# TensorE in program order in a banded attention loop, with background work shared out by key tiles

## The chip, the cores and the metric

The kernel runs on one core of a Trainium2 chip. The metric is the device time of one execution in microseconds; three runs were timed, and one more was profiled.

## The reference

The reference is a backbone of four layers over 512 latent and 256 context tokens of width 1024. Layer 1, where the change lies, is a banded grouped-query attention: 16 heads of 64 in 4 groups with shared keys and values, a window of 128 tokens to either side, and a sink logit for each head. Latent tokens see the band and all context tokens; context tokens see the context alone.

```python
mask = (jnp.abs(qpos[:, None] - kpos[None, :]) <= B_WINDOW) & (kpos[None, :] >= 0) & (kpos[None, :] < n)
s_band = jnp.einsum('bqhgd,bkhd->bhgqk', qi, kb).astype(jnp.float32) * scale
s_band = jnp.where(mask, s_band, NEG_INF)
s_ctx = jnp.einsum('bqhgd,bkhd->bhgqk', qi, k_c).astype(jnp.float32) * scale
return sink_attend([s_ctx, s_band], [v_c, vb], sink_l)
...
y_x = (o_x * jax.nn.silu(gate_x)) @ w_out
```

Each layer also has shift, scale and gate vectors, made by a 1024 x 3072 product of a conditioning vector (`mx = cond_x @ w_mod[layer] + b_mod[layer]`).

## The kernel before

All products run in float32 with operands split in a high and a low part, so that one product is two or three matmuls. The program is written with a planner: instructions are recorded in program order, and when the program is closed the planner simulates time and sets the order on each engine. On the chip each engine then works strictly in its own order.

`layer_B` first makes keys and values, and then loops over 96 units. A unit is one head and one block of 128 queries. There are 4 groups, 2 pairs of heads in each, 6 blocks, 2 heads of the pair: `n // 12` is the round `c`, so a round is one pair of heads over all six blocks. A latent block sees 4 or 5 key tiles of 128 (blocks 0 and 3: 4, blocks 1 and 2: 5), a context block (4 and 5) sees 2. In unit n, in this order in the program:

- `scores` of unit n + 2 (AH = 2): window scores (L1159) and masks (L1164), context scores (L1169) into one of two PSUM pairs; then on VectorE a reduce (L1174), on ScalarE the exponential with its sum (L1175), on VectorE reciprocal (L1176) and scale (L1177).
- `turn` of unit n: transposes (L1191) into one of three PSUM banks called short, then `split_ps`: ScalarE copies the high part (L337), VectorE subtracts the low part (L338).
- for the second head of a pair, `mix`: the product with the values (L1204), high parts first and then low parts, followed by two copies on ScalarE (L1207, L1208), two sums on VectorE (L1209, L1210) and a product on GpSimd (L1212).

Between these, `carry` advances a generator of background work for later rounds, before and after each `turn`: query projections (L1095) with their transposes (L1105), gate projections (L1076), and one filler per round from `CN`. A filler is a unit of the modulation product: four groups of four matmuls (L438), each group on its own 512 KB transfer from `w_mod`, then a copy on ScalarE (L469), transposes (L473) and small VectorE work (L477 to L483). The stream of these transfers (issued at L207) takes a buffer when an older one is free: in rounds 0 to 5 the first two groups of a filler have their weights loaded long ahead, and the transfers for the third and the fourth group wait on the queue until the first and the second group have been read. All background work uses one PSUM bank (called long, `pa0`), so the next piece must wait until the last one's bank has been read.

The steps of background work come from

```python
RATE = (5, 5, 5, 5, 5, 5, 5, 5)
...
carry(RATE[c] * 0.5)
turn(g, b, hh, prs.pop(0))
carry(RATE[c] * 0.5)
```

so five steps for each unit, whatever its size; rounds 0 to 5 have 47 to 49 steps.

Of the kernel before, what the change touches and what calls it, by code (L numbers as in the profile page):

```python
# [12 lines left out]
F32 = mybir.dt.float32  # L13
F32R = mybir.dt.float32r
BF16 = mybir.dt.bfloat16
AF = mybir.ActivationFunctionType
# [3 lines left out]
P = 128  # L20
# [11 lines left out]
CH = ((0, 384),)  # L32
LS = 2
WD = 3
RATE = (5, 5, 5, 5, 5, 5, 5, 5)
CN = (1, 1, 1, 1, 1, 1, 0, 9)
BK = (4, 5)
MI = (4, 8, 12, 16)
# [93 lines left out]
class Ring:  # L132
# [6 lines left out]
    def next(self):  # L139
        self.i += 1  # L140
        return self.blocks[self.i % len(self.blocks)]
# [125 lines left out]
class Kern:  # L267
# [761 lines left out]
    def layer_B(self, L, j, h, last):  # L1029
        nc, io = self.nc, self.io  # L1030
# [11 lines left out]
        BL = [1, 0, 2, 3, 4, 5]  # L1042
# [5 lines left out]
        qv = q.v(4, T)  # L1048
# [5 lines left out]
        wide, long, short = Banks(banks[0:BK[0]]), Banks(banks[BK[0]:BK[1]]), Banks(banks[BK[1]:8])  # L1054

        def taken(nm):
            ws = [self.W.take((nm, kb)) for kb in range(2)]
            return ws, lambda k: tuple(x[:, k % 4] for x in ws[k // 4][1])

        def roped(ps, t):  # L1060

            src = ps[:, 0:256].rearrange("p (h c) -> p h c", h=4)
            if t >= 4:
                return src
            rf = self.ropes.next().v(4, 64)
            self.rope_ps(rf, src, t, 4)
            return rf

        def gate(c):

            blk, (wh, wl) = self.W.take(("gate", c))
            for t0, n in spans:
                o = long.next()[:, 0:n]
                for k in range(KD):
                    for i, (l, part) in enumerate(((wh, 0), (wh, 1), (wl, 0))):
                        nc.tensor.matmul(o, l[:, k], self.h_at(h, part, k, t0, n), start=(k == 0 and i == 0), stop=(k == KD - 1 and i == 2))  # L1076
                    if k < KD - 1:
                        yield
                if t0:
                    blk.free()  # L1080
                self.gate2(ogv[:, c, t0:t0 + n], o)
                yield

        held, done = {}, []

        def query(g, t):

            if t == BL[0]:
                held[g] = taken(f"q{g}")
            ws, wk = held[g]  # L1090
            ps = long.next()
            for k in range(KD):
                wh, wl = wk(k)
                for i, (part, w) in enumerate(((0, wh), (0, wl), (1, wh))):
                    nc.tensor.matmul(ps[:, 0:256], self.h_at(h, part, k, P * t, P), w, start=(k == 0 and i == 0), stop=(k == KD - 1 and i == 2))  # L1095
                if k < KD - 1:
                    yield
            src = roped(ps, t)
            st = small.next()
            sv = st.v(4, 2, 64)  # L1100
            nc.scalar.activation(sv[:, :, 0], src, AF.Copy, scale=-0.125)
            nc.vector.scalar_tensor_tensor(sv[:, :, 1], src, -0.125, sv[:, :, 0].bitcast(F32), op0=ALU.mult, op1=ALU.subtract)  # L1102
            pt = short.next()
            for i in range(4):
                nc.tensor.transpose(pt[:, P * i:P * i + P], st.v(4, P)[:, i].bitcast(F32), self.ident)  # L1105
            nc.scalar.activation(qv[:, :, P * t:P * t + P], pt.rearrange("p (h n) -> p h n", h=4), AF.Copy)
            if t == BL[-1]:
                done.append(g)
                for blk, _ in ws:
                    blk.free()  # L1110
            yield

        def keys():

# [29 lines left out]
        def window(b):  # L1144
            return (max(0, b - 1), min(3, b + 1) + 1) if b < 4 else (0, 0)
# [36 lines left out]
        def turn(g, b, hh, pr):  # L1182
            lo, hi = window(b)
            nk = hi - lo + 2
            if hh % 2 == 0:
                ptl[0] = pts.next().v(2, 5, 256)
            ptv = ptl[0]
            for i0, n in ((0, 3), (3, 2)) if nk == 5 else ((0, nk),):
                tp = short.next()
                for i in range(n):  # L1190
                    nc.tensor.transpose(tp[:, P * i:P * i + P], pr.ap[:, P * (i0 + i):P * (i0 + i) + P], self.ident)  # L1191
                c0 = P * (hh % 2)
                self.split_ps(ptv[:, 0, i0:i0 + n, c0:c0 + P], ptv[:, 1, i0:i0 + n, c0:c0 + P],
                              tp[:, 0:P * n].rearrange("p (k n) -> p k n", k=n))
# [21 lines left out]
        def background(c):  # L1216

            g = (c + 1) // 2
            gates = gate(c + 1) if c < 7 else iter(())
            for i in range(3):  # L1220
                if g < 4:
                    yield from query(g, BL[i if c % 2 else i + 3])
                if c % 2:
                    for _ in range(KD):
                        if next(gates, 1) != 1:
                            yield
            yield from gates
            left = CN[c]
            while left and self.fillers and (self.fillers[0][0] == "ab" or self.fillers[0][1] == L):
                yield from self.unit(long.next)  # L1230
                left -= 1

        for x in [gate(0)] + [query(0, BL[i]) for i in range(3)]:
            for _ in x:
                pass
        units = [(g, b, 2 * p + i) for g in range(4) for p in range(2) for b in range(6) for i in range(2)]
        ahead = AH
        prs = [scores(*u) for u in units[:ahead]]
        debt = 0.0

        def carry(steps):
            nonlocal debt
            debt += steps
            while debt >= 1:
                debt -= 1
                next(back, None)

        for n, (g, b, hh) in enumerate(units):
            c = n // 12
            if n % 12 == 0:  # L1250
                back = background(c)
                debt = 0.0
                if c == 7:
                    assert done == [0, 1, 2, 3]
                    for x in h:
                        x.free()
                    self.ropes.free()
                    self.M.cap_d = self.M.look_d = 2
                    self.W.cap_w, self.W.cap_d = 8, 1
            if n + ahead < len(units):  # L1260
                prs.append(scores(*units[n + ahead]))
            carry(RATE[c] * 0.5)
            turn(g, b, hh, prs.pop(0))
            carry(RATE[c] * 0.5)
            if hh % 2:
                mix(g, b, hh // 2)
            if n % 12 == 11:
                assert next(back, 1) == 1, c
            self.W.pump(*((8, 8) if c == 7 else (3, 2)))
        for r in (small, pts, prob, sums):  # L1270
            r.free()
        for x in (q, kx, vb):
# [552 lines left out]
```

## Time and profile before

| what | value |
|---|---|
| median of three runs | 1970.33 us (1959.76 to 1973.29) |
| profiled execution | 1957.76 us |
| its span | 1956.0 us |
| TensorE busy | 1820.0 us (93%) |
| banded attention loop | 674 to 1016 us of the span |
| TensorE busy in the loop | 312.9 of 342 us |
| mean granted TensorE clock | 0.988 |

The span is the time from the first to the last instruction of the execution that the profiler recorded. Times inside the loop are counted from the span's start. PE is TensorE's matmuls, PEld its weight loads, DVE VectorE, ACT ScalarE, POOL GpSimd, SP the queue that issues transfers. The ends of matmuls are modelled, so that a matmul's row lasts longer than its share of the engine, and a wait shorter than the difference does not show.

### The profile page before, as it was taken

The numbers are of one execution on the slowest core, as the hardware profiler recorded it, in microseconds if no ns is written. First come the engines' busy times: TensorE is split into PE (matmuls) and PEld (weight loads), VectorE is DVE, ScalarE is ACT, GpSimd is POOL, SyncE is SP. The second block draws the span as 40 slices with busy tenths as digits, with TensorE's granted clock in tenths as the row PEclk, the third lists the DMA queues.
The fourth block names the chain that finished last, engine by engine and source line by source line (L and its number), as shares of the span: only waits on it lengthen the run. The fifth ranks groups of instructions, "written<-read, shape, count | busy, mean of one in ns | idle before, by whom it ended". The sixth has DMA issues, their size and how long they took to land. (4 is left out here: it accounts for less than half of the span.)

```text
span 1956.0 us, 30330 instructions
## 1 busy us (share of the span) xinstructions
PE 1820.0 (93%) x11628; PEld 1575.7 (81%) x11628; DVE 1176.2 (60%) x2364; ACT 813.0 (42%) x1694; POOL 521.9 (27%) x523
## 2 busy tenths in 40 slices
PE   5878999999999999999989899999998998999998
PEld 3657688999988878887858699999987777889986
DVE  6694225777746376667755455556667553477663
ACT  3473223545634255555653422222222353354451
POOL 5561000000314322222221444444444221000120
PEclk9999999999999999999989999999998999999999
DMA  7965541011222121222363622222222234310121
GB/s 221 264 181 156 163 130 32 13 33 33 78 96 87 55 76 54 76 77 87 100 202 112 195 69 69 85 76 70 73 76 93 88 118 138 102 34 22 44 76 54
DMA packets 186357, 186.32 MB, mean 95 GB/s; under 512 B 16600, under 2 KB 164952, under 8 KB 186212
## 3 DMA queue, kind: packets, MB, share of 16 engines
q1 hardware_dynamic: 186212, 184.39, 30.6%
q8 instruction: 91, 1.49, 0.3%
q14 instruction: 54, 0.44, 0.1%
HBM read 160.24 MB, written 24.12 MB: 94 GB/s over the span
## 5 line engine op out<-in xcount | busy, mean ns | idle before, releaser
L611 PE MATMUL pb<-arena_r 128*128 128x512 f32 (+1 forms) x1536 | 291.5, 344 | 7.3 <-DVE arena_f L1525 3.6
L611 PEld LDWEIGHTS pb<-arena_r 128*128 128x128 f32 x1536 | 238.4, 191 | 39.1 <-issue 4.5
L337 ACT ACTIVATE arena_r<-pa 128x384 fp32r<-128x384 f32 (+2 forms) x382 | 174.8, 479 | 208.6 <-PE pa L925 68.5
L338 DVE TENSOR_TENSOR arena_r<-pa,arena_r 128x384 fp32r<-128x384 f32 (+2 forms) x382 | 199.5, 537 | 96.8 <-ACT arena_r L337 95.1
L611 PE MATMUL pa<-arena_r,swing_R 128*128 128x512 f32 (+1 forms) x816 | 166.8, 356 | 1.1 <-ACT arena_f L454 0.5
L611 PEld LDWEIGHTS pa<-arena_r,swing_R 128*128 128x128 f32 x816 | 132.1, 188 | 25.2 <-issue 1.6
L900 PE MATMUL pb<-arena_r 128*128 128x384 f32 (+1 forms) x720 | 141.5, 337 | 3.0 <-ACT arena_r L337 1.8
L691 POOL TENSOR_TENSOR arena_f<-arena_f 128x128 f32<-128x128 f32 (+1 forms) x44 | 20.8, 473 | 408.6 <-DVE arena_f L690 223.4
L229 POOL TENSOR_TENSOR swing_R<-arena_f,swing_R 128x1024 fp32r<-128x1024 f32 (+1 forms) x33 | 76.1, 2311 | 187.3 <-ACT swing_R L226 133.1
L900 PEld LDWEIGHTS pb<-arena_r 128*128 128x128 f32 x720 | 119.0, 189 | 5.1 <-ACT arena_r L337 2.5
L645 PE MATMUL pb<-arena_r 128*128 128x512 f32 x480 | 116.6, 395 | 0.0
L645 PEld LDWEIGHTS pb<-arena_r 128*128 128x128 f32 x480 | 89.4, 188 | 21.5 <-issue 2.8
L354 POOL TENSOR_SCALAR small<-small 128x1 f32<-128x1 f32 x68 | 18.6, 274 | 326.1 <-ACT trash L587 136.6
L229 POOL TENSOR_TENSOR arena_r<-swing_F,arena_r 128x1024 fp32r<-128x1024 f32 x34 | 84.4, 2483 | 74.0 <-ACT arena_r L226 73.9
L939 PE MATMUL pa<-arena_r 128*128 128x256 f32 x624 | 91.4, 287 | 2.1 <-DVE arena_r L338 2.1
L939 PEld LDWEIGHTS pa<-arena_r 128*128 128x128 f32 x624 | 81.8, 190 | 4.7 <-ACT arena_r L337 2.5
L1095 PE MATMUL pa<-swing_R,arena_r 128*128 128x256 f32 x576 | 77.2, 285 | 3.8 <-DVE arena_f L344 2.0
L904 DVE TENSOR_REDUCE small<-pb 128x1 f32<-128x768 f32 (+1 forms) x80 | 67.5, 846 | 21.6 <-PE pb L900 20.8
L907 ACT ACTIVATE arena_f<-pb,small 128x768 f32<-128x768 f32 (+1 forms) x80 | 65.2, 816 | 33.0 <-DVE small L905 26.6
L226 ACT ACTIVATE arena_r<-swing_F 128x1024 fp32r<-128x1024 f32 x35 | 37.2, 1063 | 93.8 <-PE pb L611 86.7
L1095 PEld LDWEIGHTS pa<-swing_R,arena_r 128*128 128x128 f32 x576 | 71.0, 189 | 5.2 <-DVE arena_f L344 2.4
L1076 PE MATMUL pa<-arena_r,swing_R 128*128 128x512 f32 (+1 forms) x384 | 73.4, 341 | 1.6 <-DVE arena_r L1102 1.4
(270 smaller groups left out, 4220.3 us busy)
## 6 DMA issues: line engine op xcount, KB each, us to landing
arena_f<-in_w_mod_dram SPq DMA_DIRECT2D x93, 512.0 KB, 4.7
swing_F<-in_c_w_in_dram SPq DMA_DIRECT2D x31, 512.0 KB, 4.0
kd<-arena_f SPq DMA_DIRECT2D x48, 256.0 KB, 3.4
arena_f<-in_a_w_in_dram SPq DMA_DIRECT2D x24, 512.0 KB, 4.3
arena_f<-kd SPq DMA_DIRECT2D x16, 768.0 KB, 4.5
arena_f<-in_b_w_in_dram SPq DMA_DIRECT2D x20, 512.0 KB, 3.8
x<-arena_f SPq DMA_DIRECT2D x18, 512.0 KB, 3.3
arena_f<-in_a_w_out_dram SPq DMA_DIRECT2D x16, 512.0 KB
```

The source lines that it names most:

```text
L226: nc.scalar.activation(hi, view, AF.Copy)
L229: eng.tensor_tensor(lo, view, hi.bitcast(F32), op=ALU.subtract)
L337: self.nc.scalar.activation(hi, src, AF.Copy)
L338: self.nc.vector.tensor_tensor(lo, src, hi.bitcast(F32), op=ALU.subtract)
L611: nc.tensor.matmul(out, l, rhs(part, k, i), start=(k == 0 and q == 0), stop=(k == kt - 1 and q == 2))
L645: nc.tensor.matmul(ys[:, 512 * hf:512 * hf + 512], ov[:, part, k], wt[:, 0, 512 * hf:512 * hf + 512], start=(k == 0 and q == 0), stop=(k = ...
L900: nc.tensor.matmul(S[:, 512 * b:512 * b + w], l, r[:, k0 + w * b:k0 + w * b + w], start=(q == 0), stop=(q == 4))
L904: nc.vector.tensor_reduce(mx, Sv, axis=AX.XY, op=ALU.max)
L907: nc.scalar.activation(pr.v(nb, w), Sv, AF.Exp, bias=mx, scale=sc, accum_out=sm)
L939: nc.tensor.matmul(o[:, 0:256], vv[:, a_, kt % 3, P * hh:P * hh + P], ptv[i // nh][:, b_, i % nh], start=(i == 0 and q == 0), stop=(i == n ...
L1076: nc.tensor.matmul(o, l[:, k], self.h_at(h, part, k, t0, n), start=(k == 0 and i == 0), stop=(k == KD - 1 and i == 2))
L1095: nc.tensor.matmul(ps[:, 0:256], self.h_at(h, part, k, P * t, P), w, start=(k == 0 and i == 0), stop=(k == KD - 1 and i == 2))
```

## The change

Four things change in `layer_B`.

1. The loop over the units is put into a region in which the planner keeps TensorE's instructions in program order. The other engines and the queues are planned as before.
2. The steps of background work in a unit are proportional to its key tiles: `rate` is the number of steps of the round divided by 44, the sum of key tiles over its units. What is left after the last unit of a round is drained there.
3. A step that ends with work on the background's bank yields "rest", and `carry` then stops until its next call. What it owes is kept.
4. The transposes and the copy of a query tile are held back by four steps of background (`DEFER`).

```diff
-RATE = (5, 5, 5, 5, 5, 5, 5, 5)
+DEFER = 4
...
                 self.gate2(ogv[:, c, t0:t0 + n], o)
-                yield
+                yield "rest"
...
-            yield
+
+            def turned():
+                pt = short.next()
+                for i in range(4):
+                    nc.tensor.transpose(pt[:, P * i:P * i + P], st.v(4, P)[:, i].bitcast(F32), self.ident)
+                nc.scalar.activation(qv[:, :, P * t:P * t + P], pt.rearrange("p (h n) -> p h n", h=4), AF.Copy)
+                if t == BL[-1]:
+                    done.append(g)
+
+            yield turned
...
                 yield from self.unit(long.next)
+                yield "rest"
                 left -= 1
 
+        def deferred(steps):
+
+            late = []
+            for x in steps:
+                late = [(k - 1, f) for k, f in late]
+                while late and late[0][0] <= 0:
+                    late.pop(0)[1]()
+                if callable(x):
+                    late.append((DEFER, x))
+                    x = "rest"
+                yield x
+            for _, f in late:
+                f()
+                yield
...
             while debt >= 1:
                 debt -= 1
-                next(back, None)
-
+                if next(back, None) == "rest":
+                    break
+
+        order_pe = self.tc.manual_schedule(engines={nc.tensor.engine})
+        order_pe.__enter__()
         for n, (g, b, hh) in enumerate(units):
             c = n // 12
             if n % 12 == 0:
-                back = background(c)
+                back = deferred(background(c))
                 debt = 0.0
+                rate = (24 * (c < 7) + 16 * (c < 7) + 7 * (CN[c] > 0) + 2) / 44
...
-            carry(RATE[c] * 0.5)
+            share = rate * (window(b)[1] - window(b)[0] + 2) * 0.5
+            carry(share)
             turn(g, b, hh, prs.pop(0))
-            carry(RATE[c] * 0.5)
+            carry(share)
...
             if n % 12 == 11:
-                assert next(back, 1) == 1, c
+                for _ in back:
+                    pass
...
+        order_pe.__exit__(None, None, None)
```

The lines of the loop move down by four (L1163 is the old L1159, L1173 the old L1169, L1195 the old L1191, L1208 the old L1204, L1179 the old L1175, L1211 and L1212 the old L1207 and L1208); the query transposes go from L1105 to L1110 and their copy from L1106 to L1111.

TensorE over the filler of round 3, before. L438 is a filler group of four matmuls (x8 is two groups), L1169 context scores, L1159 and L1164 window scores and masks, L1191 transposes of the probabilities, L1105 transposes of queries:

```order
L438 MATMUL pa_65<-arena_f,cst 32x256 x8
L1169 MATMUL pb_70<-arena_r 128x256 x2
L1159 MATMUL pb_69<-arena_r 128x256
L1164 LDWEIGHTS identb
L1164 MATMUL pb_69<-maskb,identb 128x128
L1159 MATMUL pb_69<-arena_r 128x256
L1191 MATMUL pa_67<-ident,arena_f 128x128 x2
L1105 MATMUL pa_68<-ident,arena_r 128x128 x4
L1169 MATMUL pb_69<-arena_r 128x256 x2
L438 MATMUL pa_65<-arena_f,cst 32x256 x4
L1191 MATMUL pa_68<-ident,arena_f 128x128 x2
L438 MATMUL pa_65<-arena_f,cst 32x256 x4
```

The same place in the changed kernel, from the first group on:

```order
L438 MATMUL pa_65<-arena_f,cst 32x256 x4
L1195 MATMUL pa_66<-ident,arena_f 128x128 x2
L438 MATMUL pa_65<-arena_f,cst 32x256 x4
L1173 MATMUL pb_69<-arena_r 128x256 x2
L438 MATMUL pa_65<-arena_f,cst 32x256 x4
L1195 MATMUL pa_67<-ident,arena_f 128x128 x2
L438 MATMUL pa_65<-arena_f,cst 32x256 x4
L1110 MATMUL pa_68<-ident,arena_r 128x128 x4
L1208 MATMUL pa_66<-arena_r 128x256 x4
```

The four groups now stand one to a step, with two pairs of transposes and one pair of context scores between the first and the last; the window scores of the next round and the query transposes, which stood among them, come after the fourth group.

TensorE at the end of round 3 in the kernel before, from the scores of the second head of the next round's block 0 to the mix (L1204) of block 5. L473 are the filler's transposes, L1095 query projections:

```order
L1169 MATMUL pb_70<-arena_r 128x256 x2
L1204 MATMUL pa_66<-arena_r 128x256 x2
L1191 MATMUL pa_68<-ident,arena_f 128x128 x2
L473 MATMUL pa_65<-ident,arena_f 128x128 x4
L1191 MATMUL pa_67<-ident,arena_f 128x128 x4
L1204 MATMUL pa_66<-arena_r 128x256 x2
L1095 MATMUL pa_65<-swing_R,arena_r 128x256 x19
L1204 MATMUL pa_66<-arena_r 128x256 x2
```

The same place in the changed kernel:

```order
L1173 MATMUL pb_70<-arena_r 128x256 x2
L473 MATMUL pa_65<-ident,arena_f 128x128 x4
L1195 MATMUL pa_67<-ident,arena_f 128x128 x2
L1163 MATMUL pb_69<-arena_r 128x256
L1168 LDWEIGHTS identb
L1168 MATMUL pb_69<-maskb,identb 128x128
L1163 MATMUL pb_69<-arena_r 128x256
L1173 MATMUL pb_69<-arena_r 128x256 x2
L1195 MATMUL pa_68<-ident,arena_f 128x128 x2
L1208 MATMUL pa_66<-arena_r 128x256 x4
```

The high and low halves of the mix of block 5 stood apart, with transposes and nineteen query projections between; now the four matmuls stand together, directly behind the block's second pair of transposes.

ScalarE at the same place in the changed kernel, from the copy of the filler's bank (L469) to the copies of the mix of block 5 (L1211, L1212). L337 is the high part out of a transposes' bank, `pa_68` that of block 5's second head; L1179 is the exponential:

```order
L469 ACTIVATE arena_f<-pa_65 128x512
L1111 ACTIVATE arena_r<-pa_68 128x4x128
L1211 ACTIVATE arena_f<-pa_66 64x128
L1212 ACTIVATE arena_f<-pa_66 64x128
L337 ACTIVATE arena_r<-pa_67 128x2x128
L1179 ACTIVATE arena_f,small<-pb_70,small 128x513
L337 ACTIVATE arena_r<-pa_68 128x2x128
L1179 ACTIVATE arena_f,small<-pb_69,small 128x513
```

The order on ScalarE is of the same kind as before; what moved is TensorE's mix, which now meets this copy with nothing between. The queue's order of transfers for the loop is the same until the last round, where four transfers of output weights come ahead of three of `w_mod`.

More of the change, by code (lines that the diff above doesn't have):

```diff
@@ L1102, in query @@
             nc.vector.scalar_tensor_tensor(sv[:, :, 1], src, -0.125, sv[:, :, 0].bitcast(F32), op0=ALU.mult, op1=ALU.subtract)
[L1103 to L1106, printed above, removed]
             if t == BL[-1]:
-                done.append(g)
                 for blk, _ in ws:
                     blk.free()
-            yield
+            def turned():
[6 more added lines that the diff above has]
+            yield turned
         def keys():
@@ L1224, in background @@
                     for _ in range(KD):
-                        if next(gates, 1) != 1:
-                            yield
+                        x = next(gates, 1)
+                        if x != 1:
+                            yield x
             yield from gates
@@ L1230, in background @@
                 yield from self.unit(long.next)
+                yield "rest"
                 left -= 1
+        def deferred(steps):
[7 more added lines that the diff above has]
+                    x = "rest"
+                yield x
+            for _, f in late:
+                f()
+                yield
         for x in [gate(0)] + [query(0, BL[i]) for i in range(3)]:
-            for _ in x:
-                pass
+            for y in x:
+                if callable(y):
+                    y()
         units = [(g, b, 2 * p + i) for g in range(4) for p in range(2) for b in range(6) for i in range(2)]
```

## The prediction

> **What bounds the kernel now.** I read the page first, then the busy time of each engine by stretches, then TensorE's own lines around the change. From the page:
>
> ```profile
> span 1956.0 us, 30330 instructions
> PE 1820.0 (93%) x11628; PEld 1575.7 (81%) x11628; DVE 1176.2 (60%) x2364; ACT 813.0 (42%) x1694; POOL 521.9 (27%) x523
> ```
>
> TensorE is the busiest engine, so what counts is the time in which it issues nothing. The changed loop lies between 674 us (the first scores) and 1016 us. Its eight rounds of twelve units are the rows of the next view; I quote an ordinary round, the last round, and the whole loop (columns: stretch, length, busy time and instructions of each engine, granted TensorE clock, DMA share, GB/s).
>
> ```profile
> 840.30:882.80 42.50, 39.38 (x303) 34.72 (x299) 28.44 (x77) 25.29 (x66) 9.15 (x11) 1.00 0.24 75
> 966.70:1016.00 49.30, 38.87 (x292) 28.72 (x290) 34.09 (x84) 29.44 (x75) 17.13 (x14) 0.90 0.64 203
> 674.00:1016.00 342.00, 312.88 (x2416) 269.13 (x2414) 238.86 (x613) 194.55 (x508) 82.17 (x95) 0.99 0.29 90
> ```
>
> TensorE is idle for 342.0 - 312.9 = 29.1 us in the loop, 10.4 us of it in the last round (49.3 - 38.9), so 18.7 us in the first seven. That is too little: the end of a matmul is modelled and covers the start of the wait behind it. The weight loads (PEld) leave 342.0 - 269.1 = 72.9 us open, 20.6 us of it in the last round, so 52 us in the first seven; that is too much, since short loads leave gaps that cost nothing. The first seven rounds thus lose between 18.7 and 52 us now. I take the middle, **35 us, or 5 us a round**.
>
> **The change, part by part.**
>
> *TensorE keeps the program's order: the modulation fillers.* In each of the first six rounds TensorE does one filler: four groups of four matmuls (line 438), each on a 512 KB weight transfer. Only two buffers hold these weights ahead; the third and fourth transfer are issued when the first and second group have been read. TensorE's rows over one filler, and the queue's row, in the kernel before:
>
> ```profile
> 839.35 1.07 PE L438 MATMUL pa<-arena_f,cst 128*32 128x256 f32 x16
> 840.35 0.50 PE L1169 MATMUL pb<-arena_r 128*128 128x256 f32 x2
> ...
> 841.18 0.38 PE L1191 MATMUL pa<-ident,arena_f 128*128 128x128 f32 x2
> ...
> 842.44 0.51 PE L1169 MATMUL pb<-arena_r 128*128 128x256 f32 x2
> 843.60 0.64 PE L438 MATMUL pa<-arena_f,cst 128*32 128x256 f32 x8 [0.65 <-DMA arena_f<-in_w_mod_dram]
> 844.17 0.44 PE L1191 MATMUL pa<-ident,arena_f 128*128 128x128 f32 x2
> 845.78 0.64 PE L438 MATMUL pa<-arena_f,cst 128*32 128x256 f32 x8 [1.17 <-DMA arena_f<-in_w_mod_dram]
> ```
>
> ```profile
> 840.05 1.02 SPq L207 DMA_DIRECT2D arena_f<-in_w_mod_dram  x2
> ```
>
> From the first group to the fourth it takes 845.78 - 839.35 = 6.4 us, set by the two transfers that start at 840.05: the third group begins 3.55 us after that, the fourth another 2.2 us later. Before, the planner fills most of this time with scores, mask matmuls, transposes and even the next round's scores (the rows of the change show them). After, only two pairs of transposes and one pair of context scores stand between the groups. By these rows a group takes half of 840.35 - 839.35, so 0.50 us, a pair of transposes 0.22 us (half of the four in 0.44 us below) and a pair of scores 0.24 us. From the first group's start to the fourth's that is 0.50 + 0.22 + 0.50 + 0.24 + 0.50 + 0.22 = 2.2 us of work. The second group is read 0.2 us later than before, so the fourth transfer lands at about 6.6 us. TensorE must wait 6.6 - 2.2 = **4.4 us in each of six rounds, 26.4 us**. Behind the waiting matmul stand the mix of that block and the next round's scores; VectorE and ScalarE run dry, since their next work comes from those. What the fillers lose before is in this row, and is part of the 35 us:
>
> ```profile
> PE pa L438 <- DMA arena_f<-in_w_mod_dram: 6.6, 8, 1.2
> ```
>
> *TensorE keeps the program's order: the mix behind its transposes.* A mix (L1204, L1208 after) needs the high parts that ScalarE copies out of the transposes' bank (L337) and the low parts that VectorE then computes (L338). In block 5 the mix now follows its transposes directly, and the copy stands behind two exponentials on ScalarE. The durations, by form:
>
> ```profile
> L1174 DVE TENSOR_REDUCE small<-pb 128x1 f32<-128x513 f32 x32 | 21.8, 685 | 2.6 <-PE pb L1169 2.2
> L1175 ACT ACTIVATE arena_f<-pb,small 128x513 f32<-128x513 f32 x32 | 22.1, 691 | 4.6 <-DVE small L1174 4.2
> L1175 ACT ACTIVATION_READ_ACCUMULATOR arena_f<-pb,small 128x1 f32 x96 | 19.7, 205 | 0.0
> L1177 DVE TENSOR_SCALAR arena_f<-arena_f,small 128x512 f32<-128x512 f32 x32 | 20.5, 643 | 0.8
> L337 ACT ACTIVATE arena_r<-pa 128x256 fp32r<-128x256 f32 x64 | 24.5, 386 | 6.9 <-PE pa L1191 6.3
> L338 DVE TENSOR_TENSOR arena_r<-pa,arena_r 128x256 fp32r<-128x256 f32 x64 | 26.7, 418 | 0.6
> L337 ACT ACTIVATE arena_r<-pa 128x512 fp32r<-128x512 f32 x32 | 19.3, 603 | 9.3 <-PE pa L1191 8.9
> L338 DVE TENSOR_TENSOR arena_r<-pa,arena_r 128x512 fp32r<-128x512 f32 x32 | 21.9, 684 | 1.8 <-ACT arena_r L337 1.6
> L1174 DVE TENSOR_REDUCE small<-pb 128x1 f32<-128x641 f32 x32 | 26.0, 820 | 3.7 <-PE pb L1169 3.4
> L1175 ACT ACTIVATE arena_f<-pb,small 128x641 f32<-128x641 f32 x32 | 25.5, 798 | 0.5 <-DVE small L1176 0.5
> L469 ACT ACTIVATE arena_f<-pa 128x512 f32<-128x512 f32 x8 | 4.8, 597 | 3.0 <-PE pa L438 2.9
> ```
>
> The pace of TensorE is in two more rows: nineteen projections in 2.41 us, of which the last one's 0.28 us is its own, so 0.118 us each; four transposes in 0.60 us, so 0.11 each.
>
> ```profile
> 850.37 2.41 PE L1095 MATMUL pa<-swing_R,arena_r 128*128 128x256 f32 x19
> 849.12 0.60 PE L1191 MATMUL pa<-ident,arena_f 128*128 128x128 f32 x4
> ```
>
> Counted from the start of the fourth filler group, TensorE reaches the mix of block 5 after 0.50 + 0.44 (query transposes) + 0.47 (mix of block 4) + 0.53 (scores) + 0.44 (filler transposes) + 0.22 + 0.53 + 0.22 = 3.35 us. ScalarE meanwhile does the filler's copy (ends at 1.2), the query copy of the same size (1.8), the two half copies of the mix (2.4). VectorE's two halves of that sum end at 3.0 and its reduce at 3.7; ScalarE's exponential and its read end at 4.6, and the copy for block 5 at 5.0 us. The mix waits 5.0 - 3.35 = 1.65 us. VectorE then has four short operations and a low part (to 4.8), a reciprocal (4.95), a reduce (5.65), a scale (6.3) and only then the low part (6.7); the high half of the mix is done at 5.25, so there is a second wait of 1.45 us: **3.1 us in block 5**. The mix of block 0 in the next round has 1.86 us of TensorE behind its last scores (two times six projections and four transposes), while a reduce of 0.82, an exponential of 1.00 with its read, and a copy of 0.60 us must pass, with VectorE late by about 0.3 us from its scale before: a wait of about 1.05 us, and 0.3 us for the low part, so **1.35 us**. Blocks 1 to 3 have 2.5 to 4 us of background in the same place and cost nothing by this count; that cover is gone where the background is short, as in the last round.
>
> The seventh round has no filler, so block 4 meets its own copy too late: one exponential of half the length, its read and a copy against 0.7 us of cover, about 1.4 us; with 2.9 and 1.35 that round loses 5.6 us. Sum of the first seven rounds: 6 x (4.4 + 3.1 + 1.35) + 5.6 = 58.7 us, against 35 us now: **+24 us**, and from **+7** to **+40** by the two bounds of what is lost now.
>
> *Background by key tiles.* The number of steps is the same, spread over twelve units where they now run out after some ten. I cost it at nothing: the work that hides it is the scores and transposes of the same unit, and its effect on covers is in the counts above. *Rest while the bank is read* and *queries turned four steps late* take away waits that are short now and are in the 35 us; I give them no gain of their own.
>
> *The last round.* It has little background, and after the change the rest of its fillers is drained behind the last unit, beside the output projection. Four transfers of output weights move ahead of three filler transfers in the queue. If all TensorE idle of the round went, it would gain 10.4 us; if each of its four wide mixes waited as block 5 does, it would lose 4 x 3.1 = 12.4 us. I take 0, since VectorE's 34.1 us of work in this round stays. Behind the loop the output projection hides the moved fillers: +1 us.
>
> *The clock.* A long idle of TensorE is followed by half speed here, and a shorter one is not:
>
> ```profile
> 984.47 0.44 PE L1191 MATMUL pa<-ident,arena_f 128*128 128x128 f32 x2 [0.71 <-DVE arena_r L338]
> 987.50 1.44 PE L1204 MATMUL pa<-arena_r 128*128 128x256 f32 x5 [2.59 <-ACT arena_r L337]
> ...
> 1008.65 0.64 PE L438 MATMUL pa<-arena_f,cst 128*32 128x256 f32 x8 [2.22 <-DMA arena_f<-in_w_mod_dram]
> ```
>
> ```profile
> 986.60:997.00 10.40, 8.76 (x40) 8.27 (x41) 8.06 (x19) 7.98 (x19) 6.44 (x4) 0.51 0.43 126
> 1000.00:1010.00 10.00, 6.42 (x61) 4.21 (x58) 6.50 (x19) 4.97 (x14) 1.36 (x3) 1.00 0.80 246
> ```
>
> After 2.59 us the clock was 0.51 for 10.4 us; after 2.22 us it stayed at 1.00. The filler's wait of 4.4 us comes in two pieces, some 2.8 us ahead of the third group and 1.6 us ahead of the fourth. So the clock may fall, and the bounds are 0 and 6 x 10.4 x 0.49 = 31 us. Much of the slow time would lie in the waits of block 5, so I take **+6 us**, near the lower end. [...]
>
> **The sum.** +24 + 0 + 1 + 6 = +31 us. The profiled execution took 1957.76 us, so it would take 1989 us. The three runs lie at 1959.76, 1970.33 and 1973.29: their median is 12.6 us above the profiled one, so against it the sum gives 2001. I predict **1994 us**, between the two.
>
> **The rivals.** *Absorbed (same).* During the filler's wait VectorE and ScalarE catch up, and the waits of block 5 vanish too: 26.4 + 7 x 1.35 = 36 us against 35, so no change but the 1 us behind the loop: 1959 to 1972 us, I say 1966. For it speaks that VectorE is busy for only 28.4 of 42.5 us in a round; against it that block 5's chain begins at the fourth group and cannot start in the wait. *Faster.* The wait of the mixes goes because the copy comes early: it decides whether L337 is done within the cover behind the transposes. Then only the fillers' 26.4 us are left of the first seven rounds (-9) and the last round's idle goes (-10): 1939 to 1951 us, I say 1945. Against it stand the exponentials ahead of the copy on ScalarE. *Half clock.* After every filler wait the clock falls for 10.4 us: 25 us more than I counted, 2019 us. That a gap of 2.59 us was enough once speaks for it. That the change does not hold TensorE's order is excluded by the rows of the change.
>
> **How the numbers follow.** Forecast 0.48, half clock 0.14, absorbed 0.27, faster 0.11. A change under 1% (some 20 us) cannot be told from none, so slower has 0.48 + 0.14 = 0.62, same 0.27, faster 0.11. The forecast alone, by the bounds of the 35 us, runs from 1977 to 2010. The range goes from 1950, which takes in the absorbed case, to 2030, above the half clock with a low count of what is lost now; some 0.13 is left out, most of it faster.
>
> **What would show it.** In the profile after: waits of L438 for its transfers between 20 and 30 us where 6.6 us stand now, in two pieces per round; the first seven rounds 44 to 47 us long; waits of L1208 for L337 and L338, longest in block 5; clock below 1.00 in some rounds. I am wrong if the filler's waits stay under 10 us, or if rounds without fillers become shorter than 40 us.

## The result and the profile after

The changed kernel took 2063.49 us (median of four runs) against 1967.48 us for the kernel before on the same chip: a ratio of 1.048, 95% interval 1.042 to 1.053. It is slower, as forecast, but by some three times the forecast's 31 us, and 33 us above the range. One of the ten executions of e10, a kernel further below, took 5045 us; its median and its ratio are those of the other nine.

The page of the kernel after:

```profile
span 2063.4 us, 30282 instructions
PE 1870.4 (91%) x11628; PEld 1602.5 (78%) x11628; DVE 1187.9 (58%) x2364; ACT 816.4 (40%) x1694; POOL 520.2 (25%) x523
```

The span grew by 2063.4 - 1956.0 = 107.4 us with the same 11628 matmuls. Where it grew is in the busy times by stretches, cut at the first context scores that are written in a round, the first stretch at the first window scores (columns as in the prediction). First of before: rounds 0 to 5, rounds 0 to 6, the last round, the loop.

```profile
674.60:930.90 256.30, 238.68 (x1859) 207.77 (x1858) 181.05 (x468) 143.82 (x380) 56.36 (x72) 1.00 0.23 71
674.60:970.60 296.00, 277.31 (x2165) 242.69 (x2163) 208.50 (x541) 167.39 (x441) 67.13 (x83) 1.00 0.23 72
970.60:1015.40 44.80, 34.37 (x242) 25.68 (x239) 29.77 (x73) 26.62 (x64) 15.04 (x12) 0.89 0.66 212
674.60:1015.40 340.80, 311.68 (x2403) 268.37 (x2401) 238.26 (x613) 194.00 (x505) 82.17 (x95) 0.98 0.29 90
```

Then of after: round 3, rounds 0 to 5, the seventh round, the last one, the loop.

```profile
852.40:907.20 54.80, 45.08 (x310) 37.12 (x310) 31.40 (x80) 23.39 (x63) 7.76 (x13) 0.91 0.16 49
677.60:1017.40 339.80, 279.74 (x1872) 231.97 (x1871) 190.78 (x474) 148.23 (x385) 56.14 (x73) 0.87 0.18 56
1017.40:1071.00 53.60, 42.68 (x273) 37.73 (x273) 31.88 (x73) 27.70 (x67) 20.17 (x15) 0.91 0.23 69
1071.00:1110.00 39.00, 31.69 (x222) 23.33 (x222) 24.96 (x64) 20.06 (x53) 5.10 (x7) 0.91 0.48 149
677.60:1110.00 432.40, 354.11 (x2365) 293.03 (x2364) 247.62 (x609) 195.98 (x504) 81.41 (x95) 0.88 0.21 66
```

The loop takes 432.4 us in place of 340.8: +91.6. Rounds 0 to 5 give +83.5 (339.8 - 256.3), the seventh +13.9 (53.6 against 296.0 - 256.3 = 39.7), the last -5.8. Behind the loop stand another +12.8 (2063.4 - 1110.0 against 1956.0 - 1015.4), ahead of it +3.0.

TensorE's clock fell to 0.87 in rounds 0 to 5, where it was 1.00. TensorE's waits there, of after (columns: total, times, longest):

```profile
PE pa L438 <- DMA arena_f<-in_w_mod_dram: 21.6, 11, 3.3
PE pa L1095 <- DVE arena_f L344: 8.3, 6, 1.4
PE pa L1208 <- ACT arena_r L337: 7.2, 13, 0.9
PE pa L1076 <- DVE arena_r L1102: 5.1, 3, 1.7
PE pb L1173 <- DVE pb L1171: 4.7, 12, 0.8
PE pa L1076 <- DVE arena_f L344: 4.1, 3, 1.4
PE pa L1110 <- DVE arena_r L1102: 2.7, 3, 0.9
...
PE pa L438 <- DVE arena_f L344: 1.3, 3, 0.4
PE pa L1095 <- DVE arena_r L1102: 1.3, 3, 0.4
PE pa L1076 <- DVE arena_f L690: 0.9, 3, 0.3
PE pa L1208 <- DVE arena_r L338: 0.9, 4, 0.2
```

Four kinds: the fillers' transfers (21.6 us); background work, L1076, L1095, L1110 and L438 behind L344, L690 and L1102 (together 23.7 us, of which 21.0 are waits until VectorE has read the one PSUM bank, and 2.7, at L1110, for its own operand); the mixes behind their two conversions (8.1); and the context scores of block 0, which wait until VectorE has copied the sink logit into the scores' bank (L1171 to L1173, 4.7). Before, in the whole loop, the same kinds read:

```profile
PE pa L438 <- DMA arena_f<-in_w_mod_dram: 9.2, 10, 2.2
...
PE pa L1204 <- ACT arena_r L337: 3.1, 2, 2.6
...
PE pa L1204 <- DVE arena_r L338: 1.9, 5, 0.8
...
PE pa L1076 <- DVE arena_r L1102: 1.4, 4, 0.5
```

One filler of after, on TensorE and on the queue (that of round 2; the prediction's rows from 839.35 on show one of before):

```profile
835.38 0.64 PE L438 MATMUL pa<-arena_f,cst 128*32 128x256 f32 x8 [0.42 <-DVE arena_f L344]
835.95 0.44 PE L1195 MATMUL pa<-ident,arena_f 128*128 128x128 f32 x2
836.32 0.64 PE L438 MATMUL pa<-arena_f,cst 128*32 128x256 f32 x8
836.89 0.50 PE L1173 MATMUL pb<-arena_r 128*128 128x256 f32 x2
839.68 1.00 PE L438 MATMUL pa<-arena_f,cst 128*32 128x256 f32 x8 [2.29 <-DMA arena_f<-in_w_mod_dram]
840.62 0.69 PE L1195 MATMUL pa<-ident,arena_f 128*128 128x128 f32 x2
843.07 1.08 PE L438 MATMUL pa<-arena_f,cst 128*32 128x256 f32 x8 [1.76 <-DMA arena_f<-in_w_mod_dram]
```

```profile
836.08 1.85 SPq L207 DMA_DIRECT2D arena_f<-in_w_mod_dram  x3
```

Between the groups stand the two pairs of transposes and the pair of scores that the order showed, and the third group begins 839.68 - 836.08 = 3.6 us after the queue's row (3.55 before). The two idles add up to 4.05 us. And from the wait on, TensorE runs at half clock (two of the six fillers, and the 41.6 us of round 3 ahead of its filler, for contrast):

```profile
781.80:798.90 17.10, 14.49 (x65) 11.65 (x65) 6.99 (x20) 6.29 (x16) 0.91 (x2) 0.50 0.23 69
839.80:850.00 10.20, 7.93 (x39) 5.16 (x37) 2.77 (x11) 2.58 (x7) 0.46 (x1) 0.50 0.48 148
852.40:894.00 41.60, 34.59 (x257) 29.91 (x256) 26.58 (x64) 18.68 (x50) 7.30 (x12) 1.00 0.09 26
```

### The profile page after: what moved, and what is told of

It is laid out like the page before. It is cut to its first block, busy times and chain, and to the rows that moved or that the text cites. A ratio compares the mean times of both kernels' runs of the same rounds, so it can differ in the third digit from the quotient of the medians.

```text
span 2063.4 us, 30282 instructions
## 1 busy us (share of the span) xinstructions
PE 1870.4 (91%) x11628; PEld 1602.5 (78%) x11628; DVE 1187.9 (58%) x2364; ACT 816.4 (40%) x1694; POOL 520.2 (25%) x523
## 5 line engine op out<-in xcount | busy, mean ns | idle before, releaser
L338 DVE TENSOR_TENSOR arena_r<-pa,arena_r 128x384 fp32r<-128x384 f32 (+2 forms) x382 | 198.9, 537 | 120.2 <-ACT arena_r L337 118.9
L337 ACT ACTIVATE arena_r<-pa 128x384 fp32r<-128x384 f32 (+2 forms) x382 | 173.5, 478 | 235.5 <-PE pa L925 68.2
L611 PE MATMUL pa<-arena_r,swing_R 128*128 128x512 f32 (+1 forms) x816 | 166.8, 355 | 1.1 <-ACT arena_f L454 0.5
L1095 PE MATMUL pa<-swing_R,arena_r 128*128 128x256 f32 x576 | 87.9, 295 | 13.9 <-DVE arena_f L344 10.1
L1076 PE MATMUL pa<-arena_r,swing_R 128*128 128x512 f32 (+1 forms) x384 | 83.4, 358 | 14.1 <-DVE arena_r L1102 7.0
L1179 ACT ACTIVATE arena_f<-pb,small 128x513 f32<-128x513 f32 (+2 forms) x96 | 62.8, 655 | 70.4 <-DVE small L1178 70.1
L1095 PEld LDWEIGHTS pa<-swing_R,arena_r 128*128 128x128 f32 x576 | 76.5, 196 | 16.9 <-DVE arena_f L344 11.7
L1178 DVE TENSOR_REDUCE small<-pb 128x1 f32<-128x513 f32 (+2 forms) x96 | 61.7, 645 | 40.8 <-PE pb L1173 39.7
L1216 POOL TENSOR_TENSOR arena_f<-arena_f 128x128 f32<-128x128 f32 x48 | 22.3, 464 | 241.8 <-DVE arena_f L1214 226.7
```

What stands on the lines that cost most here:

```text
L337: self.nc.scalar.activation(hi, src, AF.Copy)
L338: self.nc.vector.tensor_tensor(lo, src, hi.bitcast(F32), op=ALU.subtract)
L611: nc.tensor.matmul(out, l, rhs(part, k, i), start=(k == 0 and q == 0), stop=(k == kt - 1 and q == 2))
L1178: nc.vector.tensor_reduce(m, src, axis=AX.X, op=ALU.min)
L1179: nc.scalar.activation(pr.ap[:, 0:P * nk + 1], src, AF.Exp, bias=m, scale=-1.0, accum_out=es)
L1216: nc.gpsimd.tensor_tensor(osl, smv[:, 1], osl, op=ALU.mult)
```

## The experiments

Theory at the start: TensorE's written order alone makes the kernel slower, by waits for the fillers' transfers, by the half clock behind them, and by waits for VectorE and ScalarE. Rivals: the new sharing of the background does it; or the waits are all one, a chain through VectorE and ScalarE that any order of TensorE meets. Each run stands beside runs of the kernel before on the same chip (medians 1963 to 1967 us).

| run | median, us | ratio to before (95%) | rounds 0 to 5, us |
|---|---|---|---|
| after | 2063.5 | 1.048 (1.042 to 1.053) | 339.8 |
| e1 order alone | 2129.8 | 1.085 (1.081 to 1.089) | 391.5 |
| e2 without the order | 1956.3 | 0.996 (0.994 to 0.998) | 245.8 |
| e8 sharing alone | 1961.8 | 0.999 (0.998 to 1.000) | |
| e4 idle filled | 2043.4 | 1.040 (1.035 to 1.044) | 316.2 |
| e3 weights held | 2020.4 | 1.028 (1.025 to 1.032) | 291.1 |
| e5 held, longer rest | 2011.7 | 1.024 (1.021 to 1.026) | 288.2 |
| e6 held, one sink copy | 2006.3 | 1.021 (1.019 to 1.024) | 287.0 |
| e9 held, late mix | 2001.2 | 1.019 (1.016 to 1.022) | 282.4 |
| e10 held, all mends | 1963.0 | 1.000 (0.999 to 1.002) | 253.5 |
| e7 order in blocks 0 to 3 | 2006.6 | 1.021 (1.018 to 1.024) | 286.7 |
| e11 no order, late mix | 1956.3 | 0.997 (0.995 to 0.998) | |
| e12 filler first | 1980.1 | 1.008 (1.005 to 1.011) | 270.0 |
| e13 filler early | 1995.6 | 1.017 (1.015 to 1.020) | 276.9 |

The runs stem from several chips, on which the kernel before differs by up to 5 us, so a difference between two medians of this table is uncertain by some us.

**The change in its parts.** e1 is the kernel before with the order alone:

```diff
+        order_pe = self.tc.manual_schedule(engines={nc.tensor.engine})
+        order_pe.__enter__()
         for n, (g, b, hh) in enumerate(units):
...
+        order_pe.__exit__(None, None, None)
```

> The kernel before, with one thing of the change: TensorE keeps the program's order in the loop. Five steps of background per unit, no rest, queries turned at once. Theory (the order is the cause: in it every wait of TensorE holds up all that stands behind): at least as slow as the whole change, 2050 to 2120 us, since five steps per unit leave the last units of a round without cover and each step meets the background's bank still being read. Rival (the new sharing of the background is the cause, the order costs little): 1965 to 2000 us.

e2 is the kernel after without these three lines.

> The changed kernel with TensorE's order left to the planner again; sharing by key tiles, rest and late queries stay. Theory (order is the cause): back to 1955 to 1985 us, loop of 335 to 355 us, half clock in the loop under 20 us. Rival (sharing is the cause): 2020 us or more.

e8 is the kernel before with `RATE[c] * 0.5` replaced by the share by key tiles, alone.

> The kernel before, with one thing of the change: background steps in proportion to key tiles, the rest drained at a round's end. The planner orders TensorE; no rest, queries turned at once. Theory (the sharing is what makes the change without the order faster than before, 0.9956): 1950 to 1962 us. Rival (the gain came from the rest or the late queries, or only from another plan): 1963 to 1985 us.

The order is the cause: with it alone the kernel is 8.5% slower, above even the upper end that was expected, and without it the rest of the change is 0.4% faster than before. The sharing alone makes no difference; which of the rest and the late queries makes e2's 0.4% wasn't tried. The two largest waits of e1 in the loop:

```profile
PE pa L1105 <- DVE arena_r L1102: 48.7, 21, 3.0
PE pa L438 <- DMA arena_f<-in_w_mod_dram: 40.0, 16, 13.2
```

Here the query transposes stand directly behind the conversion that they read (48.7 us); in the loop of after, where they are turned four steps late and the background rests, 3.0 us of that are left. So the other three parts of the change mend what the order costs, 1.085 to 1.048, but not all of it.

**The fillers and the clock.** e3 takes the transfers away: groups 3 and 4 of the fillers of rounds 0 to 5 read the weights of groups 1 and 2 again.

```diff
+            if (L, c) in HELD and kb > 1:
+                blk, w = kept[kb - 2]
```

> The changed kernel, but in the fillers of rounds 0 to 5 the third and fourth group read the weights of the first and second again: two of four transfers are left out (so half of that product is computed with other weights), and the groups stand where they stood. The order of TensorE is the same. Theory clock (the fillers' waits bring TensorE to half speed, and that costs more than the waits themselves): the waits of the fillers (22 us idle in the loop) go, half clock in the loop falls from 102 us to under 30 us, and the time falls by 50 to 75 us, to 1990 to 2015 us. Rival waits (the half clock lies in waits and costs nothing by itself): the time falls by 22 to 33 us, to 2030 to 2042 us.

e4 leaves the transfers and fills the idle with matmuls whose result nothing reads, 20 ahead of group 3 and 8 ahead of group 4:

```diff
+                    if c < 6 and i in WARM:
+                        spare = short.banks[short.i % len(short.banks)]
+                        for _ in range(WARM[i]):
+                            nc.tensor.matmul(spare[:, 0:256], kxv[:, 0, 0, 0:P], kxv[:, 0, 0, 0:256], ...)
```

> The changed kernel with 20 extra matmuls ahead of the third filler group and 8 ahead of the fourth, in rounds 0 to 5, into a bank that is overwritten next; they only keep TensorE at work where it waits for the transfers (0.118 us each at full clock, 2.4 and 0.9 us). The transfers land when they did. Theory clock: half clock in the loop falls from 102 us to under 35 us and the time by 25 to 45 us, to 2018 to 2040 us, although the fillers' weights come no sooner. Rival waits: no change or a few us more, 2055 to 2075 us.

Rounds 0 to 5 of e4, and of e3:

```profile
684.00:1000.20 316.20, 272.25 (x2040) 232.90 (x2039) 189.45 (x473) 148.37 (x384) 56.11 (x73) 0.99 0.20 61
678.60:969.70 291.10, 251.15 (x1872) 211.30 (x1871) 189.11 (x473) 147.13 (x385) 56.09 (x73) 0.99 0.15 44
```

In e4 the transfers still set when a group can begin (5.1 us of waits for them are left), but the clock is back at 0.99: 339.8 - 316.2 = **23.6 us** were the clock (20 us in the medians, just under the 25 expected). From e4 to e3 the transfers themselves go: 316.2 - 291.1 = **25.1 us**, 4.2 us a round. e3's 43 us lie between what the two theories gave, since one priced the clock too high and the other at nothing. What is left against before, 291.1 - 256.3 = **34.8 us**, is neither transfer nor clock. The kernel before itself waits for these transfers, 6.6 us in the same rounds, so against it without them the rest would be larger by up to that.

**What is left.** Three mends on top of e3, each alone. e5 rests over two calls of `carry` in place of one:

```diff
+            if pause:
+                pause = False
+                return
```

> The kernel of the run with held filler weights (two of four filler transfers left out in rounds 0 to 5; 2020 us), and the background rests over two calls of carry in place of one after a step whose bank must be read; what it owes is kept. Theory bank (in program order TensorE stands before the next query or gate matmul until VectorE has read the one background bank, 24 us idle in the loop at lines 1095, 1076 and 1110 of the changed kernel): these waits fall to under 12 us and the time by 10 to 20 us, to 2000 to 2010 us. Rival (VectorE is late as a whole, so the wait only moves to the mixes or to the drain at a round's end): 2015 to 2030 us, with more idle at the mixes.

e6 copies the sink for the first pair of heads only:

```diff
-            if b == 0:
+            if b == 0 and g == 0 and hh < 2:
```

> The kernel with held filler weights again, and the sink column is written by VectorE for the first pair of heads alone (later heads use its sinks, so their softmax is another); the scores of block 0 in later rounds no longer wait for that copy. Theory in-order (each wait of TensorE in order costs its own length): the 4.2 us idle at the context scores go, and with the part hidden by matmul ends 6 to 10 us, to 2010 to 2015 us. Rival (the copy is late because the exponential before it is late, and the scores wait for the bank in any case): 2017 to 2022 us.

e9 writes a mix into the next unit, ahead of its transposes:

```diff
+            if late_mix:
+                mix(*late_mix.pop())
             turn(g, b, hh, prs.pop(0))
             carry(share)
             if hh % 2:
-                mix(g, b, hh // 2)
+                late_mix.append((g, b, hh // 2))
```

> The version whose fillers read weights already on the chip for their groups 3 and 4 (its output is not the reference's for that reason), and in it the matmuls of each mix written one unit later, after the next unit's scores and its first share of background. That version took 2020 us, with 10.6 + 4.1 us of TensorE idle ahead of the mixes, for the two conversions of the probabilities. Theory (each wait of TensorE's order is lost by itself): those waits fall below 4 us and no other rises by as much, 2005 to 2012 us. Rival (the conversions on ScalarE and VectorE set the pace there, and what TensorE doesn't wait for at the mix it waits for at the next transposes or scores): the waits move, 2016 to 2026 us.

By the medians e5 won 9 us where 10 to 20 were expected, e6 14 where 6 to 10 were, and e9 19, more than the theory's 8 to 15; each against the kernel before on its own chip, they won 7, 12 and 17. In rounds 0 to 5 they won 2.9, 4.1 and 8.7 us; the rest of each gain lies outside these rounds and was not taken apart. The waits of the mixes in rounds 0 to 5 of e3, of e5 and of e9 (L1215 is L1208 of after, L338 and L339 its L337 and L338):

```profile
PE pa L1215 <- ACT arena_r L338: 8.5, 14, 0.9
...
PE pa L1215 <- DVE arena_r L339: 1.8, 6, 0.3
```

```profile
PE pa L1215 <- ACT arena_r L338: 13.1, 19, 1.1
```

```profile
PE pa L444 <- DVE arena_f L697: 6.1, 3, 2.0
...
PE pa L1215 <- DVE arena_r L339: 1.2, 5, 0.3
```

The longer rest takes the waits of the background from 23.7 to 13.6 us, and part of that moves into the mixes (13.1 us against 8.5), as its rival said; the late mix nearly ends their wait (1.2 us), but a new one of 6.1 us stands at the filler, until its bank's last reader (L697, the rope of a query) is done. So the gain of these two was partly given back, and e10, all of them together, tells whether one chain stands behind:

> All four mends in one: the fillers' groups 3 and 4 on weights already there, the sink's copy for the first pair alone (both change the output), a rest over two calls, and the late mix. Alone, on top of the first (2020 us), the second took 14 us away and the third 9. Theory (the losses of the program's order are separate waits, and add up): 2020 - 14 - 9 and 8 to 15 for the mixes, 1982 to 1990 us, with the rounds at 43 to 45 us. Rival (behind the waits stands one chain through VectorE and ScalarE, which shows up at whichever instruction is next): 1997 us or more. Were it at 1965 or below, the order itself would cost nothing once its waits are gone.

Rounds 0 to 5, and the whole loop, of e10:

```profile
677.90:931.40 253.50, 237.69 (x1868) 208.79 (x1867) 181.86 (x454) 145.85 (x380) 55.74 (x72) 1.00 0.16 49
677.90:1031.80 353.90, 322.80 (x2458) 276.10 (x2456) 243.88 (x601) 198.80 (x509) 83.21 (x97) 0.98 0.23 73
```

1963.0 us against 1963.2: the third case of the expectation, below the theory and its rival. The losses more than add up: in rounds 0 to 5 the three mends took 15.7 us away when each stood alone (2.9 + 4.1 + 8.7), and 37.6 us together (291.1 - 253.5). That fits mends that gave part of their gain back while they stood alone; it isn't shown wait by wait. No chain through VectorE and ScalarE holds these rounds above 253.5 us, 2.8 us less than the kernel before needs. So with these four waits gone the fixed order costs next to nothing against the kernel before. Against e2, which shares the background out in the same way without the order, it is still 7.7 us more in these rounds (245.8). Neither comparison is clean: e10 also lacks the transfers for which the kernel before waits (9.2 us) and most copies of the sink. e10's last round is longer (56.6 us against 44.8), and the time behind the loop shorter (1963.9 - 1031.8 = 932.1 us against 940.6 before), for the fillers of that round are now done inside it.

**Versions.** e7 keeps the order only where blocks are wide:

```diff
+            if (b < 4) != (order_pe is not None):
+                if b < 4:
+                    order_pe = self.tc.manual_schedule(engines={nc.tensor.engine})
...
+                    order_pe.__exit__(None, None, None)
```

> The changed kernel, with TensorE's order kept only while the unit is one of blocks 0 to 3; in blocks 4 and 5, where the fillers and the short mixes are, the planner orders TensorE. Theory (the fillers' waits with the clock, and the mixes of the short blocks, make the larger part): 1985 to 2015 us, half clock in the loop under 25 us, filler waits under 10 us. Rival (the order costs as much in the wide blocks, by the background's bank): 2020 to 2045 us.

It more than halves the loss, to 1.021, inside the theory's bounds. Its wait for transfers in the loop:

```profile
PE pa L438 <- DMA arena_f<-in_w_mod_dram: 10.4, 9, 5.0
```

That is half of after's, and waits of the background stay, such as L1076's. e11 is e2 with the late mix of e9:

> The changed kernel without TensorE's fixed order, which took 1956 us against 1965 before, and in it the mix written one unit later. Nothing is left out of the computation. Theory (the planner places the mixes by when their operands are ready, wherever they are written): no change, 1951 to 1962 us. Rival (a later mix in the program's order also ranks lower with the planner, and gives its slot to the next unit's scores, which start the longer chain): 1940 to 1950 us.

No difference to e2, as the theory said: where the mix is written does not matter when the planner orders TensorE. e12 and e13 look for an order that hides the transfers without leaving them out: the filler is written ahead of other background work, with a rest after each group, beside the longer rest and the late mix.

```diff
+            if c % 2:
+                yield from fill(c)
             for i in range(3):
...
+            if not c % 2:
+                for x in gates:
+                    yield x
+                    if x == "rest":
+                        break
+                yield from fill(c)
             yield from gates
```

This is e13; in e12 `fill(c)` stands first in every round.

> The whole computation, in TensorE's fixed order, with the three mends that leave nothing out: a rest over two calls, the mix one unit later, and the filler of a round written first in the round, with a rest after each of its groups, in place of last and together (rounds 0 to 5). A call of the background comes every 1.8 us (42 us for 24 calls), so the third group stands four calls, 7 us, behind the first, where its transfer lands some 4.3 us after the first group's start and the fourth about 6.4 us. Theory (the changed kernel lost its time to waits of the written order, each with a cure in the order itself): no transfer waits, no half clock in rounds 1 to 5, the sink's copy still waited for: 1964, the version with all four mends, and about 10 for the sink, 1967 to 1985 us. Rival (the filler keeps the one background bank through half of the round, so that projections bunch behind it and their waits grow): 1990 to 2010 us.

That expectation calls the computation whole. It isn't: in rounds 0, 2 and 4 scores of blocks 3 to 5 read their queries ahead of the transposes that write them, so the time lacks that dependency.

> The run before this one was meant to compute everything and did not: in rounds 0, 2 and 4 the filler stood ahead of that round's own queries, and scores of blocks 3 to 5 were written ahead of the queries that they read. Here the filler stands first only in rounds 1, 3 and 5; in rounds 0, 2 and 4 it comes behind the queries and the first half of the gate, with a rest over two calls after each group, as in the other rounds, and the late mix is kept. Everything is computed. Theory (the order's losses are waits that another written order can hide): the odd rounds as short as with held weights, 41 to 43 us; in the even rounds the filler begins some two thirds through, so that its end is drained behind the last unit with the second half of the gate, with at most one transfer wait of about 2 us: 1968 to 1990 us in all. Rival (the background bank, held by the filler for half of a round, bunches the projections): every round at 45 us or more, 1992 us or above.

e13 took 1995.6 us, 68 us less than after, in a fixed order and with every transfer, inside its rival's bounds. Its waits in rounds 0 to 5:

```profile
PE pa L1110 <- DVE arena_r L1102: 8.5, 7, 2.2
PE pa L1076 <- DVE small L477: 3.8, 3, 1.3
PE pa L438 <- DVE arena_f L344: 3.7, 3, 1.2
...
PE pa L438 <- DMA arena_f<-in_w_mod_dram: 2.0, 4, 0.8
```

The transfers' waits went from 21.6 to 2.0 us without leaving anything out, and the mean clock of its rounds is 0.99. So the transfers' price was their place in the order. But its rounds are 45 to 48 us, as the rival said: background waits stay (query transposes 8.5 us, and the filler's bank). Whether another order removes them too is open. The fastest kernels that compute everything are e2 and e11, without the order.

## Why the prediction was wrong

**What bounds the kernel.** That the loop and TensorE's idle in it set the time holds: 91.6 of 107.4 us arose there. **What failed first is the 35 us that were taken off as lost now,** as if the new waits replaced the old idle. TensorE is idle for 256.3 - 238.7 = 17.6 us in rounds 0 to 5 before, and for 253.5 - 237.7 = 15.8 us in e10, where the order's waits are mended: most of that idle isn't what the order replaces. The new waits came on top. As every loss below is measured as a difference to the kernel before, this is 35 us of the miss. How much of the old idle was replaced after all isn't known, beyond the 6.6 us of transfers that the kernel before waits for; whatever it is, the deduction was wrong by that much less, and the terms below are too small by that much more.

**Fillers, 4.4 us in each of six rounds, 26.4 us.** Right: 25.1 us by e4 and e3, in two pieces per filler.

**Mixes, 3.1 us in block 5 and 1.35 in block 0.** Too much: six rounds of these are 26.7 us, and the trace shows 8.1; the late mix won 8.7 us (291.1 - 282.4). In block 5 the mix waits 0.5 to 0.8 us a round in after, and 0.8 us in e3. In e3's round 4 its last transposes begin at 919.27, 4.7 us behind the fourth filler group (914.58), where the working had TensorE at the mix itself after 3.35; on the way stand two waits for the sink's copy. And the low part is done 0.8 us behind the copy (920.94 and 920.13), where the working had 1.7 us (6.7 and 5.0).

**"Background by key tiles" and "rest" costed at nothing, blocks 1 to 3 too: wrong.** In a fixed order the next projection stands behind the one bank that the piece before it used, and the scores and transposes of the unit, which were counted as its cover, are too short: 23.7 us in six rounds, 21.0 of them for the bank. The sink's copy, 4.7 us, isn't in the sum. The seventh round lost 13.9 us, where 5.6 were counted. Over seven rounds the terms came to 58.7 us, and 25.1 + 34.8 + 13.9 = 73.8 were measured: 15 us of the miss. That they came so near is luck, for two errors of opposite sign stand in them, the mixes and the background.

**The clock, +6 us.** Mis-sized: 23.6, inside the bounds of 0 and 31. It was put low because much of the slow time was to lie in the waits of block 5, and those are short. The half-clock rival had this right, with 31 us, but stood on the same deduction and so ended at 2019. In the row of 839.68 above, 2.29 us of idle had 10.2 us at 0.50 behind it, where the prediction went by a row of 2.59 us. The real gap is longer than the row shows, as matmul ends are modelled; with the two scores ahead of it at 0.12 us each it is an estimated 2.6 us.

**The last round 0, behind the loop +1.** -5.8 and +12.8: 6 us of the miss. Of the fillers' matmuls (L438), 64 now stand in the 60 us behind the loop, where 24 stood. Another 3.0 us lie ahead of the loop; their cause is open. Together, with 23.6 - 6 = 17.6 us for the clock, 35 + 17.6 + 15.1 + 6.0 + 3.0 = 76.7 us, which is the 76 us between +31 and +107.4.

Of the things that were to show it, the waits of L438 (21.6 us, in two pieces) and the clock came as said; the rounds of 44 to 47 us did not (54.8 in round 3), nor were the mixes' waits longest in block 5 (0.5 to 0.8 us a round there, up to 0.9 in block 0). Absorbed fell: block 5's waits are nearly as short in e3 (0.8 us), where no filler waits, so little was taken up during that wait. Faster fell too: the mixes still wait, and the other waits came on top.

## What to carry to other kernels

When an engine is put into a written order, price every place where it now stands behind its own operand or a single buffer, not only the transfers, and take nothing off for idle that the order doesn't replace. Here TensorE's waits for the fillers' transfers, 2.25 to 3.31 us at the first of each filler, had a slow clock behind them that cost about as much again (23.6 us behind 25.1), so the two have to be counted together. If an order must be fixed, put consumers a unit behind their producers and a long-latency filler where work separates its parts: here that, with a longer rest of the background, brought 1.048 to 1.017.

## What was not expected of the hardware

After each of the six fillers the clock fell, with 2.25 to 3.31 us of idle at the first of its waits, and for longer than the wait: 10.2 us after three of them and 17.1 after the others. At two other places 1.71 us of idle were followed by 3.4 us of half clock (0.50 from 703.3 to 706.7 us at the first), where behind the idle of 2.22 us in the kernel before it was 1.00 from 1008.65 to the loop's end. One of these two, and the first and the longest of the fillers' idles:

```profile
702.84 2.57 PE L1076 MATMUL pa<-arena_r,swing_R 128*128 128x512 f32 x6 [1.71 <-DVE arena_r L1102]
...
724.22 1.08 PE L438 MATMUL pa<-arena_f,cst 128*32 128x256 f32 x8 [2.25 <-DMA arena_f<-in_w_mod_dram]
...
895.44 1.08 PE L438 MATMUL pa<-arena_f,cst 128*32 128x256 f32 x8 [3.31 <-DMA arena_f<-in_w_mod_dram]
```

The longest idle didn't bring the longest slow stretch: behind 2.25 us stand 17.1 us, behind 3.31 us 10.2 us. And by these rows the half clock came behind 1.71 us, where it didn't behind 2.22 us. What sets whether the clock falls, and for how long, isn't shown here.
